# Query products of 512 columns for the last six heads of an attention layer, with the Vector engine's and the Scalar engine's work around them put in another order

## The chip, the cores and the metric

The kernel runs on one core of a Trainium2 chip. Its metric is the device time of one execution in microseconds (us), given as the median of several runs. The core has a matrix engine (PE, with its weight loads in the row PEld), a Vector engine (DVE), a Scalar engine (ACT), a GpSimd engine (POOL) and a queue that issues transfers (SP). Each takes its instructions in order and waits on semaphores for the others.

## The reference

Two pre-norm residual layers over 256 tokens of width 1024 in float32: layer 0 mixes tokens with attention, layer 1 with causal pooling, and each is followed by a squared-ReLU MLP of width 4096. The change lies in the attention of layer 0. With 256 tokens there is one block of keys, so the block choice falls away and plain causal attention is left:

```python
q, k, v = split(rms_norm(x) @ w_qkv)        # 8 heads of 128
q, k = rope(q), rope(k)                     # on the first 32 of 128 channels
p = softmax(causal(q @ k.T / sqrt(128)))
x = x + (p @ v) @ w_o
x = x + square(relu(rms_norm(x) @ w_up)) @ w_down
```

## The kernel before

**Numbers in two halves.** A float32 product is made from three products in the faster type fp32r. Each weight slab `raw` (one megabyte, 128 x 2048) is split into a high part `wh` (ACT, line 177, two pieces of 128 x 1024) and a low part `wl = raw - wh` (DVE, line 181, two pieces). The normed activations `xs` hold for each of the eight k-tiles 256 columns of high part and 256 of low part. A product is then wh·hi + wl·hi + wh·lo.

**Two forms of the product.** `chan_block` issues for a k-tile three matmuls of 256 columns into one bank of PSUM (lines 410, 411, 415). The wide form issues one of 256 columns, wl·hi (`wide_lo`, line 425), and one of 512, wh·[hi, lo] (`wide_hi`, line 432); a whole bank then holds a main term in its left half and a small term in its right half, and whoever empties the bank adds the two.

**The attention loop.** The eight heads go in four pairs, j = 0 to 3; keys and queries of a pair lie with channels on the partitions, so f = 0, 1 is the head within the pair. Before the change the keys of pairs 1 to 3 use the wide form (`key_evac`: two ACT copies of the small terms at line 615, two DVE additions at 616, a shuffle at 617, and the rotation on POOL at 620 to 622); the queries use `chan_block` and `qk_evac` (shuffle at 598 and multiplication by the cosine table at 599, both straight from PSUM, then two small operations at 601 and 602 on DVE or POOL). For j = 1, 2, 3 PE does, in this order: keys of j; within them `attend(j-2)`; `scores(j-1)`; queries of j; `prob_t(j-1)`. `scores` makes q·k, takes the negated row maxima (DVE, line 640), exponentials with sums (ACT, 648), reciprocals of the sums (DVE, 651) and scales the probabilities, those of the pair's first head on ACT (656) and of its second on DVE (659). `prob_t` transposes them on PE (670). `attend` multiplies with the values; ACT and DVE then split the output `o` into `ah` and `al` (709, 710). After the loop comes the projection with `w_o`, with `attend(2)`, `scores(3)` and `attend(3)` between its groups.

**What sets the order.** Each engine's order is the order in which the program text issues (the schedule is manual). Weight pieces are issued by `pump`, `pump_h` and `pump_l` at chosen places, one piece of `wh` on ACT and then one of `wl` on DVE. PSUM is handed round: the pool `ps_t` has two banks, taken in turn by scores `s`, transposed probabilities `pt` and outputs `o`. The scores of the second head of pair j-1 therefore wait until `al` has been read from `o` of pair j-2.

Of the kernel before, what the change touches and what calls it, by code (L numbers as in the profile page):

```python
# [11 lines left out]
F32 = mybir.dt.float32  # L12
F32R = mybir.dt.float32r
I32 = mybir.dt.int32
AF = mybir.ActivationFunctionType
ALU = mybir.AluOpType
ENG = mybir.EngineType

P = 128
SEQ = 256  # L20
# [3 lines left out]
ROT = 32  # L24
KT = D // P
NS = SEQ // P
HALF = 512
# [57 lines left out]
def tile_trunk(ctx: ExitStack, tc: tile.TileContext, x_in, positions, norm_mix, norm_mlp,  # L85
               w_qkv, w_o, pool_w, pool_scale, w_up, w_down, norm_final, consts, out):
    nc = tc.nc
# [5 lines left out]
    work = ctx.enter_context(tc.tile_pool(name="work", bufs=2))  # L93
    small = ctx.enter_context(tc.tile_pool(name="small", bufs=2))
    ps_d = ctx.enter_context(tc.tile_pool(name="ps_d", bufs=1, space=bass.MemoryType.PSUM))
    ps_u = ctx.enter_context(tc.tile_pool(name="ps_u", bufs=2, space=bass.MemoryType.PSUM))
# [90 lines left out]
    def hi_step():  # L187

        if not todo:
            i = state["next"]  # L190
            if i > min(state["cur"] + AHEAD, len(slabs) - 1):
                return False
            todo.extend(split_steps(i))
            state["next"] += 1
        step = todo.pop(0)
        step[0]()
        lows.append((state["next"] - 1, not todo, step[1]))
        return True

    def lo_step():  # L200
        if not lows:
            return False
        i, last, f = lows.pop(0)
        f()
        done[i] = done.get(i, 0) + 1
        if last:
            done[i] = 99
        return True

    def pump_h(n):  # L210
        for _ in range(n):
            hi_step()
# [5 lines left out]
    def pump(n):  # L218
        for _ in range(n):
            hi_step()  # L220
            while lows:
                lo_step()
# [182 lines left out]
    def chan_hi(acc, w, k, f, first):  # L405

        fs = slice(f * P, (f + 1) * P)
        o = acc[:, f * SEQ:(f + 1) * SEQ]
        hi = xs[:, k, 0:SEQ]
        nc.tensor.matmul(o, w[0][:, k, fs], hi, start=first, stop=False, skip_group_check=True)  # L410
        nc.tensor.matmul(o, w[1][:, k, fs], hi, start=False, stop=False, skip_group_check=True)  # L411
# [6 lines left out]
    def chan_block(acc, w, f):  # L418
        for k in range(KT):
            chan_hi(acc, w, k, f, k == 0)  # L420
            chan_lo(acc, w, k, f, k == KT - 1)

    def wide_lo(acc, w, k, f, first=True):

        nc.tensor.matmul(acc[:, 0:SEQ], w[1][:, k, f * P:(f + 1) * P], xs[:, k, 0:SEQ],  # L425
                         start=first and k == 0, stop=not first and k == KT - 1,
                         skip_group_check=True)

    def wide_hi(acc, w, k, f, first=False):


        nc.tensor.matmul(acc, w[0][:, k, f * P:(f + 1) * P], xs[:, k, :],  # L432
                         start=first and k == 0, stop=not first and k == KT - 1,
                         skip_group_check=True)
# [72 lines left out]
    for k in range(KT):  # L507
# [5 lines left out]
        for n, h in steps:  # L513
# [3 lines left out]
            for s in range(NS):  # L517
                x0 = (SEQ if n == 1 else 0) + s * P
                w = wl if n == 2 else wh
# [17 lines left out]
        if 2 <= k < 6:  # L537
# [3 lines left out]
                                 scale=1.0 / 32.0, accum_out=acc0[:, h, s:s + 1])  # L541
        if k == 5:
# [4 lines left out]
                                           op0=ALU.add, op1=ALU.add)  # L547
# [29 lines left out]
    scale = 1.0 / math.sqrt(P)  # L577
    tab = {}
# [9 lines left out]
    swap = [(i + half) % ROT for i in range(ROT)]  # L588

    def qk_bank(nm, j):  # L590
        return ps_u.tile([P, HALF], F32, tag="u", name="u_%s_%d" % (nm, j))

    def qk_evac(nm, j, u):
        ct, st = tab[nm]
        t = work.tile([P, 2, SEQ], F32, tag="X", name="t_%s_%d" % (nm, j), bufs=4)
        sw = work.tile([ROT, 2, SEQ], F32, tag="sw", name="sw_%s_%d" % (nm, j), bufs=2)
        uv = u.rearrange("p (f t) -> p f t", f=2)
        nc.vector.stream_shuffle(sw.rearrange("p f t -> p (f t)"), u[0:ROT, :], swap)
        nc.vector.tensor_tensor(t, uv, ct.broadcast_to([P, 2, SEQ]), op=ALU.mult)
        e = nc.vector if j == 0 or (nm, j) == ("q", 1) else nc.gpsimd  # L600
        e.tensor_tensor(sw, sw, st.broadcast_to([ROT, 2, SEQ]), op=ALU.mult)
        e.tensor_tensor(t[0:ROT], t[0:ROT], sw, op=ALU.add)
        return t
# [2 lines left out]
        return [ps_d.tile([P, HALF], F32, tag="d%d%d" % (f, 1 - j % 2), name="k_%d_%d" % (j, f))  # L606
                for f in range(2)]

    def key_evac(j, us):

        ct, st = tab["k"]
        t = work.tile([P, 2, SEQ], F32, tag="X", name="t_k_%d" % j, bufs=4)
        sw = work.tile([ROT, 2, SEQ], F32, tag="sw", name="sw_k_%d" % j, bufs=2)
        for f in range(2):
            nc.scalar.activation(t[:, f, :], us[f][:, SEQ:2 * SEQ], AF.Copy)
            nc.vector.tensor_tensor(t[:, f, :], us[f][:, 0:SEQ], t[:, f, :], op=ALU.add)
        nc.vector.stream_shuffle(sw.rearrange("p f t -> p (f t)"),
                                 t[0:ROT].rearrange("p f t -> p (f t)"), swap)
        e = nc.gpsimd
        e.tensor_tensor(t, t, ct.broadcast_to([P, 2, SEQ]), op=ALU.mult)  # L620
        e.tensor_tensor(sw, sw, st.broadcast_to([ROT, 2, SEQ]), op=ALU.mult)
        e.tensor_tensor(t[0:ROT], t[0:ROT], sw, op=ALU.add)
        return t

    qk = {}
    prob = {}
    mask = cst[:, C_MASK:C_MASK + 3 * P]

    def scores(j):
        q, k = qk["q", j], qk["k", j]  # L630
        pr = []
        mx = small.tile([P, 4], F32, tag="mx", name="mx_%d" % j)
        sums = small.tile([P, 4], F32, tag="sums", name="sums_%d" % j)
        for a in range(2):
            sp = ps_t.tile([P, HALF], F32, tag="t", name="s_%d_%d" % (j, a))
            nc.tensor.matmul(sp[:, 0:P], q[:, a, 0:P], k[:, a, 0:P], start=True, stop=True)
            nc.tensor.matmul(sp[:, P:3 * P], q[:, a, P:2 * P], k[:, a, :], start=True, stop=True)
            pa = work.tile([P, 3 * P], F32, tag="Y", name="p_%d_%d" % (j, a), bufs=4)
            for b, (c0, c1) in enumerate(((0, P), (P, 3 * P))):
                nc.vector.tensor_tensor_reduce(  # L640
                    pa[:, c0:c1], sp[:, c0:c1], mask[:, c0:c1], scale=-1.0, scalar=-NEG,
                    op0=ALU.add, op1=ALU.min, accum_out=mx[:, 2 * a + b:2 * a + b + 1])
            pr.append(pa)
        pump_h(1)
        for a in range(2):
            for b, (c0, c1) in enumerate(((0, P), (P, 3 * P))):
                i = 2 * a + b
                nc.scalar.activation(pr[a][:, c0:c1], pr[a][:, c0:c1], AF.Exp, scale=-1.0,
                                     bias=mx[:, i:i + 1], accum_out=sums[:, i:i + 1])
        pump_l(1)  # L650
        nc.vector.reciprocal(sums, sums)
        for a in range(2):
            for b, (c0, c1) in enumerate(((0, P), (P, 3 * P))):
                i = 2 * a + b
                if a == 0:
                    nc.scalar.activation(pr[a][:, c0:c1], pr[a][:, c0:c1], AF.Copy,
                                         scale=sums[:, i:i + 1])
                else:
                    nc.vector.tensor_scalar(pr[a][:, c0:c1], pr[a][:, c0:c1],
                                            sums[:, i:i + 1], None, op0=ALU.mult)  # L660
        prob[j] = pr

    pts = {}
# [52 lines left out]
    for j in range(4):  # L716
        w = use("k", j)
        if j == 0:
            u = qk_bank("k", j)
            chan_block(u, w, 0)  # L720
            tables()
            pump_h(2)
            v_evac(0, 0)
            v_evac(1, 0)
            chan_block(u, w, 1)
            v_evac(0, 1)
            v_evac(1, 1)
            qk["k", j] = qk_evac("k", j, u)
            pump_l(2)
        else:  # L730
            us = key_banks(j)
            for f in range(2):
                for k in range(KT):
                    wide_lo(us[f], w, k, f)
            pump(1)
            if j >= 2:
                attend(j - 2)
            for f in range(2):
                for k in range(KT):
                    wide_hi(us[f], w, k, f)  # L740
            qk["k", j] = key_evac(j, us)
            scores(j - 1)
        w = use("q", j)
        u = qk_bank("q", j)
        chan_block(u, w, 0)
        pump(1 if j else 2)
        chan_block(u, w, 1)
        qk["q", j] = qk_evac("q", j, u)
        if j == 0:
            pump(1)  # L750
        if j == 3:
            nc.scalar.activation(vh, vsb[:, 0, HALF:D], AF.Copy)
            nc.vector.tensor_tensor(vl, vsb[:, 0, HALF:D], vh.bitcast(F32), op=ALU.subtract)
        if j >= 1:
            prob_t(j - 1)
        pump(1)
# [10 lines left out]
    w = use("o", 0)  # L767
# [6 lines left out]
    w = use("o", 1)  # L774
# [4 lines left out]
    w = use("o", 2)  # L779
# [414 lines left out]
```

## Time and profile before

| what | us |
|---|---|
| median of 3 runs (lowest, highest) | 485.41 (484.21, 485.72) |
| time of the profiled execution | 484.62 |
| its span in the profile | 482.5 |
| PE busy | 474.7 |
| DVE busy | 338.8 |
| ACT busy | 255.1 |
| POOL busy | 43.1 |

The profiled execution is 0.8 us below the median, and 2.1 us of its time lie outside the span. In a row of the timeline the first number is the start in us from the span's start, the second the duration; then come engine, line, operation, output and inputs with their sizes, and in brackets the idle time before it with what ended it. A PE row's duration overlaps the next row's, since matmuls are pipelined; the distance of two starts is what a matmul costs.

### The profile page before, as it was taken

To read this page: it belongs to the slowest core of one execution; us is meant where nothing else is said; L and a number is where in the kernel's file an instruction comes from. 1 tells how busy PE (TensorE), PEld (TensorE's weight loads), DVE (VectorE), ACT (ScalarE), POOL (GpSimd) and SP (SyncE) were. 2 spreads that over 40 slices of the span, in tenths; PEclk is the share of its full clock that TensorE was granted. 3 is DMA by queue.
4 is the path that set the end of the run, shared out by engine and by line. 5 is a ranking of instruction groups with operands and counts; after the bars stand their busy time and mean duration, and the time that the engine had idled before them with its cause. 6 is when DMAs were issued, how large, how long until landed. Compare 5 with 4: busy or idle time off the path is not lost.

```text
span 482.5 us, 6552 instructions
## 1 busy us (share of the span) xinstructions
PE 474.7 (98%) x2570; PEld 412.1 (85%) x2570; DVE 338.8 (70%) x498; ACT 255.1 (53%) x418; POOL 43.1 (9%) x41
## 2 busy tenths in 40 slices
PE   8999999999999999999999999999999999999994
PEld 7789999888888888888888889888888888888884
DVE  4789998955877484848566687778756557484745
ACT  4696665653686272635355554476535446272523
POOL 6910456300000000000000000000000000000000
PEclk9999999999999999999999999999999999999999
DMA  7986643480477758556573570078747472736202
GB/s 266 349 280 223 196 174 123 143 259 1 124 251 236 263 196 282 186 163 219 170 249 147 175 261 2 18 248 297 239 135 277 139 252 97 262 120 230 88 1 87
DMA packets 57342, 89.58 MB, mean 186 GB/s; under 512 B 2944, under 2 KB 46048, under 8 KB 57312
## 3 DMA queue, kind: packets, MB, share of 16 engines
q1 hardware_dynamic: 56896, 88.72, 55.1%
q8 instruction: 20, 0.33, 0.3%
q10 hardware_dynamic: 416, 0.45, 0.3%
q14 instruction: 10, 0.08, 0.0%
HBM read 88.11 MB, written 1.05 MB: 185 GB/s over the span
## 4 chain that ended last, share of the span: by engine, by line
PE 97%; DMA 1%; SPq 0%; ACT 0%; DVE 0%; issue 0%; ACTq 0%
PE u_m L432 24%; PE u_m L425 13%; PE d_m L401 12%; PE d_m L402 12%; PE d_m L403 12%; PE d_v L520 4%; PE k L432 2%; PE u_q L411 2%; PE u_q L410 2%; PE u_q L415 2%; PE d_o L401 2%; PE d_o L403 2%; PE d_o L402 2%; DMA xt<-in_x_dram 1%; PE k L425 1%; PE d_p L1066 1%
## 5 line engine op out<-in xcount | busy, mean ns | idle before, releaser
L432 PE MATMUL u_m<-xs,wh_u 128*128 128x512 f32 x512 | 122.1, 390 | 0.0
L432 PEld LDWEIGHTS u_m<-xs,wh_u 128*128 128x128 f32 x512 | 94.7, 188 | 18.8
L401 PE MATMUL d_m<-wh_d,hh 128*128 128x512 f32 x252 | 98.1, 389 | 0.0
L402 PE MATMUL d_m<-wl_d,hh 128*128 128x512 f32 x252 | 98.0, 389 | 0.0
L403 PE MATMUL d_m<-wh_d,hl 128*128 128x512 f32 x252 | 98.0, 389 | 0.0
L181 DVE TENSOR_TENSOR wl_d<-raw_d,wh_d 128x1024 fp32r<-128x1024 f32 x64 | 76.2, 1221 | 17.0 <-ACT wh_d L177 17.0
L181 DVE TENSOR_TENSOR wl_u<-raw_u,wh_u 128x1024 fp32r<-128x1024 f32 x64 | 75.8, 1222 | 12.2 <-ACT wh_u L177 12.2
L177 ACT ACTIVATE wh_d<-raw_d 128x1024 fp32r<-128x1024 f32 x64 | 64.7, 1046 | 21.7 <-DMA raw_d<-in_mlp_w_down_dram 21.7
L799 ACT ACTIVATE t<-u_m 128x256 f32<-128x256 f32 x64 | 24.0, 378 | 83.8 <-PE u_m L425 54.6
L177 ACT ACTIVATE wh_u<-raw_u 128x1024 fp32r<-128x1024 f32 x64 | 63.9, 1046 | 7.1 <-DMA raw_u<-in_mlp_w_up_dram 7.1
L425 PEld LDWEIGHTS u_m<-xs,wl_u 128*128 128x128 f32 x512 | 64.0, 191 | 1.4
L425 PE MATMUL u_m<-xs,wl_u 128*128 128x256 f32 x512 | 64.9, 283 | 0.0
L800 DVE TENSOR_TENSOR t<-u_m,t 128x256 f32<-128x256 f32 x64 | 26.5, 422 | 53.9 <-ACT t L799 53.2
L403 PEld LDWEIGHTS d_m<-wh_d,hl 128*128 128x128 f32 x252 | 47.3, 188 | 9.8
L401 PEld LDWEIGHTS d_m<-wh_d,hh 128*128 128x128 f32 x252 | 47.3, 188 | 9.8
L402 PEld LDWEIGHTS d_m<-wl_d,hh 128*128 128x128 f32 x252 | 47.3, 188 | 9.8
L810 ACT ACTIVATE hh<-hf 128x512 fp32r<-128x512 f32 x32 | 20.2, 633 | 45.0 <-DVE hf L809 45.0
L811 DVE TENSOR_TENSOR hl<-hf,hh 128x512 fp32r<-128x512 f32 x32 | 22.2, 692 | 22.5 <-ACT hh L810 22.5
L809 DVE SCALAR_TENSOR_TENSOR hf<-t 128x512 f32<-128x512 f32 x32 | 22.1, 692 | 1.1
L410 PE MATMUL u_q<-xs,wh_q 128*128 128x256 f32 x64 | 18.6, 291 | 0.0
L411 PE MATMUL u_q<-xs,wl_q 128*128 128x256 f32 x64 | 18.1, 283 | 0.0
L415 PE MATMUL u_q<-xs,wh_q 128*128 128x256 f32 x64 | 18.1, 283 | 0.0
(218 smaller groups left out, 554.8 us busy)
## 6 DMA issues: line engine op xcount, KB each, us to landing
raw_u<-in_mlp_w_up_dram SPq DMA_DIRECT2D x32, 1024.0 KB, 6.3
raw_d<-in_mlp_w_down_dram SPq DMA_DIRECT2D x32, 1024.0 KB, 4.8
raw_o<-in_attn_w_o_dram SPq DMA_DIRECT2D x4, 1024.0 KB, 4.8
raw_k<-in_attn_w_qkv_dram SPq DMA_DIRECT2D x4, 768.0 KB, 5.2
raw_q<-in_attn_w_qkv_dram SPq DMA_DIRECT2D x4, 768.0 KB, 4.8
raw_v<-in_attn_w_qkv_dram SPq DMA_DIRECT2D x2, 1024.0 KB, 9.0
raw_v<-in_attn_w_qkv_dram SPq DMA_DIRECT2D x3, 512.0 KB, 7.1
raw_k<-in_attn_w_qkv_dram SPq DMA_DIRECT2D x4, 256.0 KB, 5.4
```

Of the source, the lines that this page charges most:

```text
L177: nc.scalar.activation(wh[:, sl], src[:, sl], AF.Copy)
L181: nc.vector.tensor_tensor(wl[:, sl], src[:, sl], wh[:, sl].bitcast(F32), op=ALU.subtract)
L401: nc.tensor.matmul(acc, lh, wh, start=first, stop=False)
L402: nc.tensor.matmul(acc, lh, wl, start=False, stop=False)
L403: nc.tensor.matmul(acc, ll, wh, start=False, stop=last)
L410: nc.tensor.matmul(o, w[0][:, k, fs], hi, start=first, stop=False, skip_group_check=True)
L411: nc.tensor.matmul(o, w[1][:, k, fs], hi, start=False, stop=False, skip_group_check=True)
L415: nc.tensor.matmul(acc[:, f * SEQ:(f + 1) * SEQ], w[0][:, k, fs], xs[:, k, SEQ:2 * SEQ], start=False, stop=last, skip_group_check=True)
L425: nc.tensor.matmul(acc[:, 0:SEQ], w[1][:, k, f * P:(f + 1) * P], xs[:, k, 0:SEQ], start=first and k == 0, stop=not first and k == KT - 1, ...
L432: nc.tensor.matmul(acc, w[0][:, k, f * P:(f + 1) * P], xs[:, k, :], start=first and k == 0, stop=not first and k == KT - 1, skip_group_che ...
L799: nc.scalar.activation(t[:, ts], u[:, SEQ:2 * SEQ], AF.Copy)
L800: nc.vector.tensor_tensor(t[:, ts], u[:, 0:SEQ], t[:, ts], op=ALU.add)
```

## The change

The queries of pairs 1 to 3 are made in the wide form, into two banks, and emptied by a new function `query_evac` in the way of the keys. ACT's copies of the small terms are in a function of their own (`small_terms`). In `scores(j-1)` the row maxima now come first on DVE, and the additions and shuffle of the keys of pair j, which stood ahead of them, follow (the argument `between`). The probabilities of both heads of a pair are scaled on ACT.

```diff
+    def small_terms(nm, j, us):
+        t = work.tile([P, 2, SEQ], F32, tag="X", name="t_%s_%d" % (nm, j), bufs=4)
+        for f in range(2):
+            nc.scalar.activation(t[:, f, :], us[f][:, SEQ:2 * SEQ], AF.Copy)
+        return t
+
-    def key_evac(j, us):
+    def key_evac(j, us, t):
...
-        t = work.tile([P, 2, SEQ], F32, tag="X", name="t_k_%d" % j, bufs=4)
         sw = work.tile([ROT, 2, SEQ], F32, tag="sw", name="sw_k_%d" % j, bufs=2)
         for f in range(2):
-            nc.scalar.activation(t[:, f, :], us[f][:, SEQ:2 * SEQ], AF.Copy)
             nc.vector.tensor_tensor(t[:, f, :], us[f][:, 0:SEQ], t[:, f, :], op=ALU.add)
...
+    def query_evac(j, us):
+
+        ct, st = tab["q"]
+        t = small_terms("q", j, us)
+        sw = work.tile([ROT, 2, SEQ], F32, tag="sw", name="sw_q_%d" % j, bufs=2)
+        for f in range(2):
+            nc.vector.tensor_tensor(t[:, f, :], us[f][:, 0:SEQ], t[:, f, :], op=ALU.add)
+        nc.vector.stream_shuffle(sw.rearrange("p f t -> p (f t)"),
+                                 t[0:ROT].rearrange("p f t -> p (f t)"), swap)
+        nc.vector.tensor_tensor(t, t, ct.broadcast_to([P, 2, SEQ]), op=ALU.mult)
+        e = nc.vector if j == 1 else nc.gpsimd
+        e.tensor_tensor(sw, sw, st.broadcast_to([ROT, 2, SEQ]), op=ALU.mult)
+        e.tensor_tensor(t[0:ROT], t[0:ROT], sw, op=ALU.add)
+        return t
...
-    def scores(j):
+    def scores(j, between=None):
...
             pr.append(pa)
+        if between is not None:
+            between()
         pump_h(1)
...
-                if a == 0:
-                    nc.scalar.activation(pr[a][:, c0:c1], pr[a][:, c0:c1], AF.Copy,
-                                         scale=sums[:, i:i + 1])
-                else:
-                    nc.vector.tensor_scalar(pr[a][:, c0:c1], pr[a][:, c0:c1],
-                                            sums[:, i:i + 1], None, op0=ALU.mult)
+                nc.scalar.activation(pr[a][:, c0:c1], pr[a][:, c0:c1], AF.Copy,
+                                     scale=sums[:, i:i + 1])
...
-            qk["k", j] = key_evac(j, us)
-            scores(j - 1)
+            t = small_terms("k", j, us)
+            scores(j - 1, lambda: qk.update({("k", j): key_evac(j, us, t)}))
         w = use("q", j)
-        u = qk_bank("q", j)
-        chan_block(u, w, 0)
-        pump(1 if j else 2)
-        chan_block(u, w, 1)
-        qk["q", j] = qk_evac("q", j, u)
         if j == 0:
...
+        else:
+            us = [ps_u.tile([P, HALF], F32, tag="u", name="q_%d_%d" % (j, f)) for f in range(2)]
+            for f in range(2):
+                for k in range(KT):
+                    wide_lo(us[f], w, k, f)
+            pump(1)
+            for f in range(2):
+                for k in range(KT):
+                    wide_hi(us[f], w, k, f)
+            qk["q", j] = query_evac(j, us)
```

On the Vector engine, at the scores of pair 0 in the turn of j = 1, the additions for the keys `t_k` (from the PSUM banks `k_0`, `k_1`) stand ahead of the maxima `mx` of the scores `s`. Before:

```order
L616 TENSOR_TENSOR t_k_587<-k_0_549,t_k_587 128x256
L616 TENSOR_TENSOR t_k_587<-k_1_550,t_k_587 128x256
L617 STREAM_SHUFFLE sw_k_588<-t_k_587 32x512
L640 ISA p_0_602,mx_597<-s_0_599,cst 128x128
L640 ISA mx_597 128x1
```

At the same place now:

```order
L659 ISA p_1_601,mx_590<-s_1_598,cst 128x256
L659 ISA mx_590 128x1
L620 TENSOR_TENSOR t_k_587<-k_0_549,t_k_587 128x256
L620 TENSOR_TENSOR t_k_587<-k_1_550,t_k_587 128x256
L621 STREAM_SHUFFLE sw_k_604<-t_k_587 32x512
```

The three operations for the keys moved behind all the maxima of the pair.

The Vector engine again, directly behind that: the second piece of the low weights of the queries of pair 2 (`wl_q`), the reciprocals, the first piece for the keys of pair 3 (`wl_k`), and the emptying of the queries of pair 1. Before:

```order
L181 TENSOR_TENSOR wl_q_568<-raw_q_473,wh_q_567 128x1024
L651 RECIPROCAL sums_598<-sums_598 128x4
L659 TENSOR_SCALAR p_1_608<-p_1_608,sums_598 128x128
L659 TENSOR_SCALAR p_1_608<-p_1_608,sums_598 128x256
L181 TENSOR_TENSOR wl_k_650<-raw_k_507,wh_k_649 128x1024
L598 STREAM_SHUFFLE sw_q_678<-u_q_624 32x512
L599 TENSOR_TENSOR t_q_677<-u_q_624,ct_q 128x512
L601 TENSOR_TENSOR sw_q_678<-sw_q_678,st_q 32x512
L602 TENSOR_TENSOR t_q_677<-t_q_677,sw_q_678 32x512
```

At the same place now:

```order
L181 TENSOR_TENSOR wl_q_568<-raw_q_473,wh_q_567 128x1024
L672 RECIPROCAL sums_591<-sums_591 128x4
L181 TENSOR_TENSOR wl_k_643<-raw_k_507,wh_k_642 128x1024
L635 TENSOR_TENSOR t_q_662<-q_0_624,t_q_662 128x256
L635 TENSOR_TENSOR t_q_662<-q_1_625,t_q_662 128x256
L636 STREAM_SHUFFLE sw_q_665<-t_q_662 32x512
L638 TENSOR_TENSOR t_q_662<-t_q_662,ct_q 128x512
L640 TENSOR_TENSOR sw_q_665<-sw_q_665,st_q 32x512
L641 TENSOR_TENSOR t_q_662<-t_q_662,sw_q_665 32x512
```

The two scalings are gone, two additions came in, and the shuffle and the multiplication read SBUF where they read PSUM.

On the Scalar engine, at the same place of the turn of j = 1, from the scaling of the probabilities `p` on. Before:

```order
L656 ACTIVATE p_0_602<-p_0_602,sums_598 128x128
L656 ACTIVATE p_0_602<-p_0_602,sums_598 128x256
L177 ACTIVATE wh_k_649<-raw_k_507 128x1024
L681 ACTIVATE pts_0_687<-pt_0_683 128x384
L681 ACTIVATE pts_1_693<-pt_1_689 128x384
```

At the same place now:

```order
L676 ACTIVATE p_0_595<-p_0_595,sums_591 128x128
L676 ACTIVATE p_0_595<-p_0_595,sums_591 128x256
L676 ACTIVATE p_1_601<-p_1_601,sums_591 128x128
L676 ACTIVATE p_1_601<-p_1_601,sums_591 128x256
L177 ACTIVATE wh_k_642<-raw_k_507 128x1024
L612 ACTIVATE t_q_662<-q_0_624 128x256
L612 ACTIVATE t_q_662<-q_1_625 128x256
L698 ACTIVATE pts_0_676<-pt_0_672 128x384
L698 ACTIVATE pts_1_682<-pt_1_678 128x384
```

Two more scalings stand ahead of the weight piece `wh_k`, and two copies of query terms stand between it and the copies `pts` of the transposed probabilities. In the turns of j = 2 and 3 the three places look alike, with pieces of `w_o` for those of the keys; there the last two operations of the query emptying are on POOL, before and now.

More of the change, by code (lines that the diff above doesn't have):

```diff
@@ L740, in tile_trunk @@
                     wide_hi(us[f], w, k, f)
-            qk["k", j] = key_evac(j, us)
-            scores(j - 1)
+            t = small_terms("k", j, us)
+            scores(j - 1, lambda: qk.update({("k", j): key_evac(j, us, t)}))
         w = use("q", j)
-        u = qk_bank("q", j)
-        chan_block(u, w, 0)
-        pump(1 if j else 2)
-        chan_block(u, w, 1)
-        qk["q", j] = qk_evac("q", j, u)
-        if j == 0:
-            pump(1)
+        if j == 0:
+            u = qk_bank("q", j)
+            chan_block(u, w, 0)
+            pump(2)
+            chan_block(u, w, 1)
+            qk["q", j] = qk_evac("q", j, u)
+            pump(1)
+        else:
[8 more added lines that the diff above has]
+            qk["q", j] = query_evac(j, us)
         if j == 3:
```

## Prediction

> **What bounds the kernel now.** First I read the busy times and the chain that ended last.
>
> ```profile
> PE 474.7 (98%) x2570; PEld 412.1 (85%) x2570; DVE 338.8 (70%) x498; ACT 255.1 (53%) x418; POOL 43.1 (9%) x41
> PE 97%; DMA 1%; SPq 0%; ACT 0%; DVE 0%; issue 0%; ACTq 0%
> ```
>
> PE is the bound, over the whole span. Next, whom PE waited for:
>
> ```profile
> PE warm_up L298 <- DVE warm L237: 1.1, 1, 1.1
> PE tr_a L318 <- DMA xt<-in_x_dram: 0.5, 1, 0.5
> ```
>
> Both waits lie before 10 us. Behind them PE never waits, so the change can gain only what it takes off PE's own work, and loses every wait that it opens. Whether one opens is read from the stage it touches:
>
> ```profile
> 55.40:70.10 14.70, 14.70 (x105) 13.83 (x104) 13.96 (x26) 8.85 (x21) 5.82 (x4) 1.00 0.51 185
> ```
>
> This is the turn of j = 2 (columns: stretch, length, busy PE, PEld, DVE, ACT, POOL, then the granted clock): DVE is busy 13.96 of 14.70 us. Over the span it has 30% to spare, here 5%; I therefore follow DVE's queue.
>
> **The change on PE.**
>
> ```profile
> 49.12 0.28 PE L411 MATMUL u_q<-xs,wl_q 128*128 128x256 f32 x1
> ...
> 54.62 0.28 PE L415 MATMUL u_q<-xs,wh_q 128*128 128x256 f32 x1
> ```
> ```profile
> 55.64 1.92 PE k L425 x16
> ...
> 58.87 3.66 PE k L432 x16
> ```
>
> These are the second and the last of the 48 query matmuls of pair 1: 46 steps in 5.50 us, 0.1196 us each, 5.74 for 48. The wide form does the same for keys in 1.92 + 3.66 = 5.58 (chain, 16 of each). Gain 0.16 a turn, 0.5 us over three. Emptying into two banks costs PE nothing: the turn between two query blocks covers it.
>
> **The change on DVE, turn of j = 1.**
>
> ```profile
> 49.68 0.74 DVE L616 TENSOR_TENSOR t_k<-k,t_k 128x256 f32<-128x256 f32 x2
> ...
> 50.46 0.72 DVE L617 STREAM_SHUFFLE sw_k<-t_k 32x512 f32<-32x512 f32 x1
> 51.09 0.26 DVE L640 CUSTOM_DVE_ANT_0 p<-s,cst 128x128 f32<-128x128 f32 x1
> ...
> 52.18 1.46 DVE L181 TENSOR_TENSOR wl_q<-raw_q,wh_q 128x1024 fp32r<-128x1024 f32 x1
> ...
> 53.77 1.38 DVE L659 TENSOR_SCALAR p<-p,sums 128x128 f32<-128x128 f32 x2
> 55.55 1.81 DVE L181 TENSOR_TENSOR wl_k<-raw_k,wh_k 128x1024 fp32r<-128x1024 f32 x1 [0.41 <-ACT wh_k L177]
> ...
> 57.29 0.72 DVE L598 STREAM_SHUFFLE sw_q<-u_q 32x512 f32<-32x512 f32 x1
> 57.92 0.66 DVE L599 TENSOR_TENSOR t_q<-u_q,ct_q 128x512 f32<-128x512 f32 x1
> ...
> 59.21 0.68 DVE L602 TENSOR_TENSOR t_q<-t_q,sw_q 32x512 f32<-32x512 f32 x1
> 59.82 1.21 DVE L181 TENSOR_TENSOR wl_k<-raw_k,wh_k 128x1024 fp32r<-128x1024 f32 x1
> ...
> 62.09 0.67 DVE L710 TENSOR_TENSOR al<-o,ah 128x512 fp32r<-128x512 f32 x1
> ```
> ```profile
> 51.27 1.29 POOL L620 TENSOR_TENSOR t_k<-t_k,ct_k 128x512 f32<-128x512 f32 x1 [16.38 <-DVE sw_k L617]
> 52.52 2.27 POOL L621 TENSOR_TENSOR sw_k<-sw_k,st_k 32x512 f32<-32x512 f32 x1
> 54.86 1.41 POOL L622 TENSOR_TENSOR t_k<-t_k,sw_k 32x512 f32<-32x512 f32 x1
> ...
> 71.29 1.28 POOL L601 TENSOR_TENSOR sw_q<-sw_q,st_q 32x512 f32<-32x512 f32 x1 [1.83 <-DVE sw_q L598]
> ```
> ```profile
> 53.77 0.80 ACT L656 ACTIVATE p<-p,sums 128x128 f32<-128x128 f32 x2 [0.51 <-DVE sums L651]
> 54.47 1.04 ACT L177 ACTIVATE wh_k<-raw_k 128x1024 fp32r<-128x1024 f32 x1
> ```
>
> DVE and POOL take turns. The `wl_q` piece starts at 52.18, POOL's first operation ends at 52.56, the piece 1.08 later (53.64); POOL's second, begun at 52.52, ends 1.15 after that (54.79), though such an operation takes 1.28 alone. The `wl_k` piece of 55.55 ends 1.09 after POOL's third (56.27). What began first goes first, the other waits for its end.
>
> The Trainium skill (page "SBUF — State Buffer", section "SBUF: two separate sides") says that GpSimd and a Vector operation with two SBUF inputs hold a shared port pair exclusively for the whole instruction, the first to start winning. The trace agrees (1.08 and 1.09 us after the other's end). Were the port shared by halves instead, `wl_k` would start at once and last at most its 1.81 us, some 0.5 late in place of 1.0, and the sum below would be nearer +3.6 than +5.0.
>
> The maxima put first shift the pieces, not their sum: `wl_q` is again at 52.18. POOL's first operation, now released only by the shuffle's end there, comes behind it, so the piece takes about 1.22 and ends at W = 53.40. Then:
> - ACT starts 0.13 after W (53.64 to 53.77), scales four pieces in 1.40 instead of two in 0.70 (53.77 to 54.47), makes `wh_k` in 1.04; DVE may begin `wl_k` 0.04 later, W + 2.61 = 56.01. Its own scaling (1.38) is gone, but DVE only idles in its place.
> - POOL's three: W + 1.15 to 1.29, 1.24 more (1.28 less the 0.04 overlap of 52.56 and 52.52), 0.07 between (54.79 to 54.86): the third starts at W + 2.46 to 2.60, up to 0.15 us ahead of `wl_k`. POOL first is likelier; `wl_k` then waits for 1.28 us of POOL and is about 1.0 late. DVE first: nothing lost.
> - Queued behind `wl_k` on DVE are the emptying of the queries, two weight pieces and `al`; for `al` PE waits.
> - The queries' emptying took 57.29 to 59.82, 2.53 us. Now: additions 0.78 (49.68 to 50.46), shuffle 0.75, multiplication 0.60 to 0.63, two small ones 1.31: 3.44. The multiplication reads SBUF now; its bounds are 0.66 (PSUM) and the 0.69 of
>
> ```profile
> L809 DVE SCALAR_TENSOR_TENSOR hf<-t 128x512 f32<-128x512 f32 x32 | 22.1, 692 | 1.1
> ```
>
> So the operation behind `wl_k` starts at 57.15 (DVE first) or 58.17 (POOL first) instead of 57.29; after 3.44 of emptying and 2.27 of two weight pieces (59.82 to 62.09) `al` ends at 63.53 or 64.55 instead of 62.76. That matters because of one moment on PE:
>
> ```profile
> 54.74 0.90 PE L670 MATMUL pt<-ident,p 128*128 128x128 f32 x6
> ...
> 63.02 0.39 PE L636 MATMUL s<-t_k,t_q 128*128 128x128 f32 x2
> 63.24 0.60 PE L637 MATMUL s<-t_k,t_q 128*128 128x256 f32 x2
> ```
>
> The second head's scores (63.02) take the PSUM bank that `al` empties; 63.02 less 62.76 leaves a slack of 0.26 us. PE comes 0.16 earlier, at 62.86, and waits **0.7 or 1.7 us**.
>
> Two smaller delays in this turn I set at nothing. The transposes of the probabilities (54.74, now about 54.58) need the last scaled piece near the end of their 0.65 us; ACT has it at W + 0.13 + 1.5 = 55.0, so PE waits between 0 and 0.1. ACT's query copies stand ahead of `pts`, which only `attend` of the next turn reads, some 2.8 us after the transposes begin; that covers them, and if it didn't it would be 0.2 at most.
>
> **Turns of j = 2 and 3.**
>
> ```profile
> 66.94 1.38 DVE L659 TENSOR_SCALAR p<-p,sums 128x128 f32<-128x128 f32 x2
> ...
> 70.48 0.73 DVE L598 STREAM_SHUFFLE sw_q<-u_q 32x512 f32<-32x512 f32 x1
> ...
> 71.80 4.09 DVE L181 TENSOR_TENSOR wl_o<-raw_o,wh_o 128x1024 fp32r<-128x1024 f32 x2
> 75.81 0.68 DVE L710 TENSOR_TENSOR al<-o,ah 128x512 fp32r<-128x512 f32 x1
> ...
> 85.03 0.72 DVE L598 STREAM_SHUFFLE sw_q<-u_q 32x512 f32<-32x512 f32 x1
> ...
> 87.95 0.74 DVE L676 TENSOR_TENSOR ptp<-pt,ptp 128x256 fp32r<-128x256 f32 x2
> ```
> ```profile
> 77.61 0.38 PE L636 MATMUL s<-t_k,t_q 128*128 128x128 f32 x2
> ...
> 88.80 0.60 PE L693 MATMUL o<-pts,vsb 128*128 128x128 f32 x4
> ```
>
> From `al`'s end to the next W lie 3.9 us (0.9 for PE's second head, 0.35 its last maximum, 0.78 + 0.64 for the keys, 1.22 for the piece). W comes at 67.4 or 68.4, the operation behind `wl_o` at W + 3.74 (71.15) or W + 4.77 (73.2) against 70.48. From there to `al`'s end it was 6.01 (to 76.49); additions and order add 0.8, a multiplication that now takes turns with POOL about 0.4: 7.2. `al` ends at 78.35 or 80.4; PE arrives at 77.61 - 0.32 + 0.7 (1.7) = 78.0 or 79.0: wait **0.4 or 1.4**.
>
> In turn 3 W is at 82.2 or 84.3, the next operation at 85.95 or 89.05 (85.03 before). The split `ptp` ended 3.66 later (88.69), now 4.8: 90.7 or 93.8. `attend(2)`, whose slack was 0.11, arrives at 88.80 - 0.48 + 1.1 (3.1) = 89.4 or 91.4: wait **1.3 or 2.4**. Later DVE waits for PE again,
>
> ```profile
> 106.97 0.69 DVE L792 TENSOR_TENSOR xt<-d_o,xt 128x512 f32<-128x512 f32 x1 [2.78 <-PE d_o L403]
> ```
>
> so nothing more is lost, nor given back.
>
> **Sum.** POOL first: 1.7 + 1.4 + 2.4 - 0.5 = +5.0. DVE first: 0.7 + 0.4 + 1.3 - 0.5 = +1.9. Both stand against the profiled execution, 484.62; the median lies 0.8 higher, which I leave inside the range. Forecast: 489.6.
>
> **Rivals.**
> 1. DVE wins the turns: +1.9, 486.5. For it: the margin is between 0.15 us and nothing. If the three turns differ, about +3.
> 2. No slower: the scaling taken from DVE (1.38) pays for the longer emptying (0.91), and `al` ends before 62.86, with all waits gone: 484.62 - 0.5 = 484.1. It decides if `wl_k` can start by about W + 1.9, as at 55.55. Against it: ACT's queue has the four scalings in front of `wh_k`, 0.70 us more.
> 3. Clearly faster, by 1.5 us and more: PE's matmuls of 512 columns would have to save three times what the keys' rows show. Nothing speaks for it.
>
> **How the numbers follow.** POOL first 0.50, mixed turns 0.13, rival 1 0.17, rival 2 0.17, rival 3 0.03. About 0.3% (1.5 us) is what a measurement can tell from no change. Slower: 0.50 + 0.13 and 0.10 of rival 1 = 0.73; same: 0.07 + 0.17 = 0.24; faster 0.03. The range leaves out rivals 2 and 3: from 485.2, below rival 1 with its waits a little smaller, to 491.2, the forecast with the median's 0.8 and POOL's longer times. Within the likeliest case alone I would say 488.4 to 491.2.
>
> **What would show it.** Right: PE idle before the second head's scores in turns 2 and 3 and before `attend(2)`, released by DVE; DVE idle over 2 us behind each reciprocal, released by ACT's weight piece; POOL's third operation starting just ahead of `wl_k`. Wrong: PE without waits and 0.5 us shorter, or a gap at the transposes of the probabilities, which I put at under 0.3 us.

## The result, and the profile after

The kernel after takes 491.62 us (median of 6 executions, 490.13 to 492.38) against 485.27 (6, 484.21 to 485.72) of the kernel before beside it: a ratio of 1.0134, 95% interval 1.0113 to 1.0154. It is slower, by more than forecast: 489.6 was said, with a range that ended at 491.2. The profiled execution took 490.13, 5.5 us more than that of before, where the sum had said 5.0.

The busy times and the chain that ended last, of the kernel after:

```profile
PE 475.2 (97%) x2522; PEld 408.5 (84%) x2522; DVE 336.2 (69%) x496; ACT 259.3 (53%) x432; POOL 41.6 (9%) x41
PE 86%; DVE 8%; ACT 2%; DMA 2%; issue 1%; SPq 0%; DVEq 0%; ACTq 0%
```

PE's busy time is nearly that of before (474.7), so the 5.5 us are not work of PE; DVE now holds 8% of the chain. Whom PE waited for (us in total, times, longest), without the waits before 10 us:

```profile
PE s L655 <- DVE al L727: 2.4, 2, 1.6
PE o L710 <- DVE ptp L693: 2.1, 1, 2.1
...
PE s L655 <- POOL t_q L641: 0.6, 1, 0.6
```

The timeline has them in these places (the idle time before a row stands in brackets):

```profile
64.26 0.49 PE L655 MATMUL s<-t_k,t_q 128*128 128x128 f32 x2 [1.61 <-DVE al L727]
...
78.91 0.49 PE L655 MATMUL s<-t_k,t_q 128*128 128x128 f32 x2 [0.62 <-POOL t_q L641]
...
80.59 0.49 PE L655 MATMUL s<-t_k,t_q 128*128 128x128 f32 x2 [0.76 <-DVE al L727]
...
93.97 0.71 PE L710 MATMUL o<-pts,vsb 128*128 128x128 f32 x4 [2.11 <-DVE ptp L693]
```

And the turn in which they arise, DVE, then POOL, then ACT:

```profile
51.82 1.20 DVE L181 TENSOR_TENSOR wl_q<-raw_q,wh_q 128x1024 fp32r<-128x1024 f32 x1
52.94 0.16 DVE L672 RECIPROCAL sums<-sums 128x4 f32<-128x4 f32 x1
55.61 2.25 DVE L181 TENSOR_TENSOR wl_k<-raw_k,wh_k 128x1024 fp32r<-128x1024 f32 x1 [2.52 <-ACT wh_k L177]
57.78 0.74 DVE L635 TENSOR_TENSOR t_q<-q,t_q 128x256 f32<-128x256 f32 x2
...
63.53 0.67 DVE L727 TENSOR_TENSOR al<-o,ah 128x512 fp32r<-128x512 f32 x1
```
```profile
51.99 2.17 POOL L624 TENSOR_TENSOR t_k<-t_k,ct_k 128x512 f32<-128x512 f32 x1 [17.75 <-DVE sw_k L621]
54.13 1.28 POOL L625 TENSOR_TENSOR sw_k<-sw_k,st_k 32x512 f32<-32x512 f32 x1
55.49 1.29 POOL L626 TENSOR_TENSOR t_k<-t_k,sw_k 32x512 f32<-32x512 f32 x1
```
```profile
53.13 1.50 ACT L676 ACTIVATE p<-p,sums 128x128 f32<-128x128 f32 x4 [1.66 <-DVE sums L672]
54.54 1.04 ACT L177 ACTIVATE wh_k<-raw_k 128x1024 fp32r<-128x1024 f32 x1
```

W, the end of the `wl_q` piece, is 53.02. ACT scales until 54.6 and only then makes `wh_k`; DVE idles 2.52 us; POOL's third operation begins at 55.49, 0.12 ahead of `wl_k`, which therefore lasts 2.25 us instead of 1.20. The emptying of the queries begins at 57.78. The same picture stands in the other two turns (`wl_o` at 71.09 and at 87.43; each takes 2.25 us and stands behind 2.51 of idleness).

### The profile page after: what moved, and what is told of

Same layout as the page of the kernel before. It is cut to its first block, busy times and chain, and to the rows that moved or that the text cites. A ratio compares the mean times of both kernels' runs of the same rounds, so it can differ in the third digit from the quotient of the medians.

```text
span 488.1 us, 6474 instructions
## 1 busy us (share of the span) xinstructions
PE 475.2 (97%) x2522; PEld 408.5 (84%) x2522; DVE 336.2 (69%) x496; ACT 259.3 (53%) x432; POOL 41.6 (9%) x41
## 3 DMA queue, kind: packets, MB, share of 16 engines
HBM read 88.11 MB, written 1.05 MB: 183 GB/s over the span
## 4 chain that ended last, share of the span: by engine, by line
PE 86%; DVE 8%; ACT 2%; DMA 2%; issue 1%; SPq 0%; DVEq 0%; ACTq 0%
PE u_m L432 24%; PE u_m L425 13%; PE d_m L403 12%; PE d_m L401 12%; PE d_m L402 12%; PE d_v L520 5%; DVE wl_o L181 2%; DVE wl_k L181 2%; PE d_o L401 1%; PE d_o L403 1%; PE d_o L402 1%; DVE wl_q L181 1%; DMA raw_q<-in_attn_w_qkv_dram 1%; ACT p L676 1%; PE pb L1010 1%
## 5 line engine op out<-in xcount | busy, mean ns | idle before, releaser
L181 DVE TENSOR_TENSOR wl_o<-raw_o,wh_o 128x1024 fp32r<-128x1024 f32 x8 | 14.3, 1797 | 5.3 <-ACT wh_o L177 5.3
L520 PE MATMUL d_v<-wh_v,xs 128*128 128x512 f32 x64 | 16.8, 400 | 0.3 <-ACT wh_v L177 0.2
L364 ACT ACTIVATE junk<-xt 128x512 f32<-128x512 f32 x15 | 9.5, 630 | 13.9 <-DVE xt L821 13.5
```

Source lines behind the costliest of these rows:

```text
L181: nc.vector.tensor_tensor(wl[:, sl], src[:, sl], wh[:, sl].bitcast(F32), op=ALU.subtract)
L520: nc.tensor.matmul(dv[s, h], xs[:, k, x0:x0 + P], w[:, k % 2, hs], start=k == 0 and n == 0, stop=k == KT - 1 and n == 2)
```

## The experiments

Each ratio is to runs of the kernel before on the same chip. The theory: DVE is late at the queries' emptying, because behind each reciprocal it waits for ACT's weight piece and then for POOL, and the longer emptying leaves nothing to make it up; PE pays for it in three places. The chief rival: the wide products in two banks are the cost themselves.

### Undoing what makes DVE late

**e1: the weight piece ahead of the scalings** (against after).

```diff
         nc.vector.reciprocal(sums, sums)
+        if between is not None:
+            pump_h(1)
         for a in range(2):
...
                     wide_lo(us[f], w, k, f)
-            pump(1)
+            pump_l(1)
```

(The second place is the one between the two passes of the queries.)

> The kernel after with one thing moved: ScalarE's piece of the next slab (wh_k in the first block) is issued between the exponentials and the four scalings, where ScalarE idles 1.66 us in the trace, instead of behind the scalings. Nothing else differs. Theory (DVE's 2.5 us of idleness behind each reciprocal is what makes DVE late, and PE waits 1.9 + 1.9 + 2.4 us for it): wl_k begins right behind the reciprocal, some 2.5 us earlier against W, the three waits fall to under 0.5 us together, and the gain of the wide queries (0.55) is left: 484.5 to 485.8 us, a ratio to before of 0.998 to 1.002. Rival (the wide products in two banks and the longer emptying are the cost, whatever DVE does behind the reciprocal): the waits at the scores and at attend(2) stay near their size, 489.5 us or more, ratio 1.009 or more.

Measured: 486.05 us, ratio 1.0025 (1.0016 to 1.0034), 0.25 us above the theory's range and far from the rival's 489.5. The edit did not do quite what was written of it: weight pieces may run only three slabs ahead, so in the first block nothing could be issued at the new place and `wl_k` came behind the emptying; in the other two blocks a `wl` piece directly follows the reciprocal. In all three the emptying now begins 1.83 us behind the reciprocal's end, instead of 4.68. What is left of PE's waits:

```profile
PE o L712 <- DVE ptp L695: 0.6, 1, 0.6
...
PE s L655 <- DVE al L729: 0.2, 1, 0.2
```

So of the 6.5 us above before (1.34% of 484.7) 1.3 are left: some 5.2 us go with DVE's lateness, while the wide products and their two banks are unchanged.

**e2: without POOL's third operation on the keys** (against after; line 626 is left out, so the keys lack one term).

```diff
-        e.tensor_tensor(t[0:ROT], t[0:ROT], sw, op=ALU.add)
```

> The kernel after without POOL's third operation on the keys (t_k plus sw_k, 32x512), so the rotated part of the keys lacks its second term. Nothing else differs. Theory (that operation, 0.12 us ahead of wl_k in each of the three blocks, holds wl_k up by 1.04 us): wl_k takes 1.20 us and not 2.25, still 2.5 us behind the reciprocal, and each of the three waits falls by about 1.0: 488.2 to 489.2 us against 491.6, ratio 1.006 to 1.008. Rival (DVE's lateness comes from ScalarE alone, the meeting with POOL lies beside other work): the waits stay, 491 to 492 us, ratio 1.012 or more.

Measured: 487.20 us, ratio 1.0052 (1.0038 to 1.0065), a larger fall than the theory's. DVE's idleness is that of after, but the piece is not held up (the timeline, then PE's waits):

```profile
56.13 1.23 DVE L181 TENSOR_TENSOR wl_k<-raw_k,wh_k 128x1024 fp32r<-128x1024 f32 x1 [2.51 <-ACT wh_k L177]
```
```profile
PE s L654 <- DVE al L726: 1.2, 2, 0.6
PE o L709 <- DVE ptp L692: 1.1, 1, 1.1
```

PE's waits at these places fall from 5.1 to 2.3 us in the trace, as expected, and the two profiled executions lie 2.7 us apart (490.13 and 487.41). The medians lie further apart because the median of after is 1.5 us above its profiled execution, which the part on the prediction takes up.

**e3: one scaling of four back on DVE** (against after).

```diff
-                nc.scalar.activation(pr[a][:, c0:c1], pr[a][:, c0:c1], AF.Copy,
-                                     scale=sums[:, i:i + 1])
+                if i != 2:
+                    nc.scalar.activation(pr[a][:, c0:c1], pr[a][:, c0:c1], AF.Copy,
+                                         scale=sums[:, i:i + 1])
+                else:
+                    nc.vector.tensor_scalar(pr[a][:, c0:c1], pr[a][:, c0:c1],
+                                            sums[:, i:i + 1], None, op0=ALU.mult)
```

> The kernel after with one of the four scalings (the second head's 128 columns) on DVE again, behind the reciprocal where DVE idles. ScalarE's piece then ends about 0.35 to 0.40 us earlier, so wl_k can begin near W+2.2 us, ahead of POOL's third operation at W+2.47. Theory (who begins first has the turn): wl_k takes 1.20 us and DVE is through at W+3.4 instead of W+4.84, each wait falls by about 1.4: 487 to 488 us, ratio 1.0035 to 1.0065. Rival (the order of beginning does not decide, POOL's operation goes first or the two share): DVE gains only the 0.4 us, each wait falls by 0.4 at most: 490 to 491.2 us, ratio 1.009 to 1.012.

Measured: 486.38 us, ratio 1.0041 (1.0028 to 1.0055); 1.65 us above before. The turns change hands:

```profile
55.59 1.23 DVE L181 TENSOR_TENSOR wl_k<-raw_k,wh_k 128x1024 fp32r<-128x1024 f32 x1 [1.07 <-ACT wh_k L177]
...
55.76 2.19 POOL L626 TENSOR_TENSOR t_k<-t_k,sw_k 32x512 f32<-32x512 f32 x1
```

DVE's piece begins 0.17 us ahead and takes 1.23; now POOL's operation takes 2.19. ACT's piece comes 0.3 us sooner against W, and the emptying begins 1.3 us sooner (W + 3.45 instead of W + 4.76). This kernel is close to the prediction's first rival: +1.9 was worked out for it.

**e4: the outputs in another bank** (against after).

```diff
-        o = ps_t.tile([P, HALF], F32, tag="t", name="o_%d" % j)
+        o = (ps_d if j < 2 else ps_t).tile([P, HALF], F32, tag="d0%d" % (j % 2) if j < 2 else "t",
+                                           name="o_%d" % j)
```

> The kernel after with the outputs of attend(0) and attend(1) in a bank of ps_d that the previous keys have left, instead of the ps_t bank that the second head's scores want next. Nothing else differs; DVE does the same work in the same order. Theory (DVE is late, the bank is only where PE meets it): the waits of the second head's scores for al (1.9 and 1.0) go, but PE then meets the late DVE elsewhere, at the third block's first scores (t_q, 1.5 or so) and at attend(2) (2.4 to 2.7): 489.6 to 491 us, ratio 1.008 to 1.012. Rival (the ring of two ps_t banks is the cost): the two waits go for good, 2.9 us less: 488.9 us or less, ratio 1.0075 or less.

Measured: 490.31 us, ratio 1.0108 (1.0092 to 1.0124): the theory's case. The waits for `al` are gone and PE meets the late DVE further on:

```profile
PE o L711 <- DVE ptp L693: 2.6, 1, 2.6
PE s L655 <- POOL t_q L641: 1.4, 1, 1.4
```

### One part of the change at a time

These start from the kernel before. e5 takes the new query branch with `query_evac` alone; e6 `between` alone; e7 the scalings alone; e8 is the kernel after without the third part (e5 and e6 together).

The core of e5, of e6 and of e7, in this order:

```diff
-        qk["q", j] = qk_evac("q", j, u)
...
+            for f in range(2):
+                for k in range(KT):
+                    wide_hi(us[f], w, k, f)
+            qk["q", j] = query_evac(j, us)
```
```diff
-            qk["k", j] = key_evac(j, us)
-            scores(j - 1)
+            t = small_terms("k", j, us)
+            scores(j - 1, lambda: qk.update({("k", j): key_evac(j, us, t)}))
```
```diff
-                else:
-                    nc.vector.tensor_scalar(pr[a][:, c0:c1], pr[a][:, c0:c1],
-                                            sums[:, i:i + 1], None, op0=ALU.mult)
...
+                nc.scalar.activation(pr[a][:, c0:c1], pr[a][:, c0:c1], AF.Copy,
+                                     scale=sums[:, i:i + 1])
```

e8 takes the last of these back in the kernel after.

> The kernel before with one part of the change alone: the queries of the last six heads by 512-column products and their longer emptying; maxima behind the keys' additions and the second head's scaling on DVE, as before. Theory (the products gain some 0.55 us, and their emptying makes DVE later by 0.9 us a block; this alone exceeds DVE's slack by a little): waits of 0.5 to 0.9 us at the second head's scores in two blocks and at attend(2), about 2.0 in sum, less the gain: 485.5 to 487 us, ratio 1.002 to 1.005. Rival (the wide products and their two banks are what costs): nearly all of it is here, 489 us or more, ratio 1.009 or more.

> The kernel before with one part alone: maxima ahead of the keys' additions, so that the keys' operations on DVE and then on POOL come about 1 us later against the exponentials; narrow queries and the second head's scaling on DVE as before. Theory: POOL's operations now meet DVE's scalings and wl_k, DVE is back some 1 us later, most of which the slack before the queries' emptying takes up; the transposes of the probabilities may wait once for about 1.3: 484.5 to 486.3 us, ratio 1.000 to 1.0035. Rival (the new order by itself is the cost): 488 us or more, ratio 1.007 or more.

> The kernel before with one part alone: all four scalings on ScalarE. DVE then idles some 2.5 us behind each reciprocal for ScalarE's piece of the next slab, as in the kernel after; but POOL's key operations, started before the maxima, are through when wl_k begins, and the short emptying leaves room. Theory (idleness costs only where POOL's operation and the longer emptying come on top): no wait of PE above 0.3 us, 484.2 to 485.4 us, ratio 0.999 to 1.0015. Rival (the scalings on ScalarE cost by themselves, wherever the rest stands): waits of 1 us or more in each block, 487 us or more, ratio 1.005 or more.

> The kernel after with the second head's two scalings on DVE again, behind the reciprocal; the wide queries and the new order of the maxima stay. ScalarE's piece ends 0.9 us earlier, but DVE's scalings now stand ahead of wl_k and meet POOL's operations. Theory: DVE is through about 3.7 us behind W instead of 4.84, each of the three waits is 0.8 to 1.2 instead of 1.9 to 2.4, and the transposes of the probabilities may wait once for about 1.3: 486.5 to 488.3 us, ratio 1.004 to 1.0075, between e5_wide_only and the kernel after. Rival (the scaling's place does not matter): 490.5 us or more, ratio 1.011 or more.

| kernel | median us | ratio to before (95%) |
|---|---|---|
| e5, wide queries | 486.75 | 1.0045 (1.0031 to 1.0059) |
| e6, maxima first | 485.15 | 1.0011 (1.0001 to 1.0021) |
| e7, scalings on ACT | 484.47 | 0.9999 (0.9988 to 1.0009) |
| e8, e5 and e6 | 486.88 | 1.0049 (1.0032 to 1.0065) |

All four times came as the theory had them, and no part alone is the culprit: 2.2, 0.5 and 0.0 us, where all three cost 6.5. In the traces PE waits 0.59, 0.31 and 0.79 us at the three places in e5, once 0.90 at the transposes in e6, nowhere in e7, and 0.37 and 0.89 at two of the three places and 0.85 at the transposes in e8. The row that shows best why is from e7:

```profile
55.91 1.23 DVE L181 TENSOR_TENSOR wl_k<-raw_k,wh_k 128x1024 fp32r<-128x1024 f32 x1 [2.51 <-ACT wh_k L177]
```

The very idleness of 2.51 us that is so dear in the kernel after is here, and costs nothing: POOL's key operations started before the maxima and are through, `wl_k` takes 1.23, and the short emptying leaves room. The parts are dear together: the scalings make the hole, the order of the maxima puts POOL's third operation at its end, and the longer emptying takes the room in which DVE would have caught up. This account is put together from e2, e3, e7 and e8; the scalings with only one of the other two parts were not run. e2, which has the hole and the longer emptying without POOL at the hole's end, stands at 1.0052, near e5's 1.0045.

### The clock behind a wait

The trace of e4 had a row that no step of the prediction had foreseen: behind the wait for `ptp` the granted clock (of PE) stood at 0.50 for some 3.4 us. The mean clock of e4's executions went with their time (0.993 and 0.994 at 491.1; 0.997 and 0.998 at 489.5 and 489.1). e10 to e12 follow that up. e10 is the kernel after again; e11 and e12 are the kernel before with one delay on DVE ahead of the third split of probabilities (six and four splits of the upper value rows; the diff is e11's):

```diff
-            nc.vector.tensor_tensor(vl, vsb[:, 0, HALF:D], vh.bitcast(F32), op=ALU.subtract)
+            for _ in range(6):
+                nc.vector.tensor_tensor(vl, vsb[:, 0, HALF:D], vh.bitcast(F32), op=ALU.subtract)
```

> The kernel after, unchanged, with more executions than the first time. Theory (in some executions the granted clock falls to half for some 3.3 us after one of PE's waits, as the trace of e4_obank shows behind attend(2); that costs about 1.7 us and lowers the mean clock of the span from about 0.998 to 0.994): the times fall into two groups, near 490 to 491.3 us at a mean clock of 0.996 or more and near 491.5 to 492.5 at 0.995 or less. Rival (the times scatter for other reasons, as those of before do): one group, and the mean clock does not go with the time.

> The kernel before with the split of the upper value rows (vl, 128x512, on DVE) written six times instead of once, so that DVE reaches the split of the third block's probabilities late and PE waits at attend(2) for about 3.6 us; nothing else differs. Theory (a wait of this length halves the granted clock for some 3.3 us afterwards): before plus 3.6, plus 0.3 to start again, plus 1.7 for the clock in nearly every execution: 489.3 to 490.8 us, ratio 1.010 to 1.013, mean clock 0.995 or less, half the clock behind the wait in the trace. Rival (the clock does not go with waiting): 487.8 to 488.8 us, ratio 1.007 to 1.009, mean clock as before.

> The same with four splits, so that PE waits at attend(2) for about 2.2 us, as in the kernel after, and nowhere else. Theory (at this length the clock falls in some executions and not in others): times in two groups, 486.6 to 487.4 us at the mean clock of before and about 1.7 us more at 0.995 or less. Rival (the clock falls at any wait of 2 us): all at 488.3 us or more; or (it falls only after some 3 us of waiting): all at 486.6 to 487.4.

e10: 491.46 us, ratio 1.0143 (1.0126 to 1.0159). With the first six there are ten executions of the kernel after: five at a mean clock of 0.994 (491.93, 491.93, 491.99, 492.27, 492.38) and five at 0.997 or 0.998 (490.13, 490.13, 491.00, 491.23, 491.24). The groups don't overlap; their means lie 1.35 us apart. Both executions of after that were profiled are of the second group, with the clock full behind waits of 2.1 us, so the low clock itself was not seen in a trace of after.

e11: 490.89 us, ratio 1.0135 (1.0121 to 1.0149), mean clock 0.991 to 0.994 in all four executions. PE waits 4.1 us instead of the 3.6 expected, and the time is 0.1 us above the theory's range and 2.1 above the rival's. e12: 489.42 us, ratio 1.0107 (1.0092 to 1.0121). Its wait came out at 2.6 us, not 2.2, and the two groups expected for it did not appear: all four stand at 0.992 to 0.994. These are PE's wait in e12, and the stretches behind it (the number ahead of the DMA share is the granted clock):

```profile
91.89 0.71 PE L693 MATMUL o<-pts,vsb 128*128 128x128 f32 x4 [2.60 <-DVE ptp L676]
```
```profile
92.00:93.00 1.00, 1.00 (x8) 1.00 (x9) 1.00 (x2) 0.00 (x0) 0.00 (x0) 0.87 0.00 0
93.00:94.00 1.00, 1.00 (x6) 0.90 (x5) 0.30 (x1) 0.29 (x1) 0.00 (x0) 0.50 0.00 0
94.00:95.00 1.00, 1.00 (x4) 0.81 (x3) 0.67 (x1) 1.00 (x2) 0.00 (x0) 0.50 0.33 85
95.00:96.00 1.00, 1.00 (x3) 0.74 (x3) 0.74 (x2) 1.00 (x2) 0.00 (x0) 0.50 0.82 220
96.00:97.00 1.00, 1.00 (x8) 0.92 (x7) 0.57 (x2) 0.19 (x1) 0.00 (x0) 0.93 0.98 312
```

If the clock is either 1.00 or 0.50, it is low for 0.26 + 3.00 + 0.14 = 3.40 us, beginning 0.85 us after PE had resumed. Read in the same way, e4 has it low for 3.40 us from 0.05 us after PE's return, and e11 for 6.8 us from 1.7 us before it. In these three traces PE had idled for 2.4 to 2.6 of the 3.4 us ahead of the fall; in the two traces of after, where the clock stayed full, for 2.1 at most. Waiting and a low clock go together, then, by the mean clocks: at 1.1 us never (e2, four executions at 0.996 or more), at 2.1 in half the executions of after, at 2.6 in six of eight (e4 and e12), at 4.1 always. The waits are those of the one or two traces of each kernel. e11 and e12 differ from before by the delay alone, so the wait is the cause there; why the same wait lowers the clock in one execution and not in another stays open.

### Whether the wide queries gain

**e9: e1, e4 and the value split moved** (against e1; the bank of e4 also in it, and the split now ahead of `query_evac`).

```diff
-        if j == 3:
+            if j == 1:
                 nc.scalar.activation(vh, vsb[:, 0, HALF:D], AF.Copy)
                 nc.vector.tensor_tensor(vl, vsb[:, 0, HALF:D], vh.bitcast(F32), op=ALU.subtract)
```

> The kernel of e1_piece_ahead with two moves more: attend(0) and attend(1) write the bank that the previous keys have left (as in e4_obank), and the split of the upper value rows (vh on ScalarE, vl on DVE) stands in the first wide block, where DVE waits 1.8 us for ScalarE, instead of the third. Theory (the 1.3 us that e1_piece_ahead is above the kernel before are its two waits left, 0.2 and 0.6 us with some 0.3 each to start again, less nothing): no wait of PE above 0.2 us at the second head's scores or attend(2), and the gain of the wide queries shows: 483.8 to 484.8 us, ratio 0.998 to 1.000. Rival (the wide queries gain nothing to speak of, or cost elsewhere): 485.2 us or more, ratio 1.001 or more.

Measured: 484.63 us against 484.37, ratio 1.0004 (0.9995 to 1.0013). PE's waits at the scores and at attend are gone, but no gain can be measured; the interval takes in both cases. The trace says more: the first scores of the first and of the fourth pair, in before and in e9:

```profile
47.69 0.38 PE L636 MATMUL s<-t_k,t_q 128*128 128x128 f32 x2
...
91.33 0.38 PE L636 MATMUL s<-t_k,t_q 128*128 128x128 f32 x2
```
```profile
47.80 0.38 PE L655 MATMUL s<-t_k,t_q 128*128 128x128 f32 x2
...
90.94 0.38 PE L655 MATMUL s<-t_k,t_q 128*128 128x128 f32 x2
```

43.64 us between them became 43.14: the 0.5 of the sum. Up to attend(3), at 101.52 and 101.29, only 0.34 is left, because DVE still idled behind the fourth reciprocal.

**e13: the piece ahead there too** (against e9).

```diff
-        if between is not None:
-            pump_h(1)
+        pump_h(1)
```

> The kernel of e9_three_moves with ScalarE's piece ahead of the scalings in the fourth pair as well, where it was left behind them. Theory (the wide queries gain 0.5 us up to the fourth pair's scores, and DVE's 2.5 us behind the fourth reciprocal give half of it back at attend(3)): attend(3) starts 53.3 to 53.4 us behind the first pair's scores instead of 53.49 (before 53.83), and the time is 0.2 to 0.3 us below e9_three_moves: 0.1 to 0.6 us below before, ratio 0.9987 to 0.9998. Rival (the gain ends in a later wait whatever attend(3) does): attend(3) starts earlier and the time is not below before, ratio 1.000 or more.

Measured: 484.54 us against 484.44, ratio 0.9994 (0.9985 to 1.0003). attend(3) stands 53.39 us behind the first scores (101.83 less 48.44), as the theory had it (before: 53.83). Of these 0.44 us another 0.2 are lost ahead of the pooling products near 288 us, where the second of two squares on ACT follows the first 0.2 us later than in before; that this is the cause was not tried, nor why it does so in e9 and e13. No kernel here beats the kernel before by what can be measured.

## Why the prediction was right, and where it was wrong

Right was the mechanism, step by step. Up to the change, the trace of after runs 0.40 us ahead of that of before (first scores at 47.29 against 47.69; PE's wait of 0.5 us for the input before 10 us is missing), so W = 53.02 is the forecast's 53.40. Forecast for ACT's start, POOL's third and `wl_k`: W + 0.13, + 2.46 to 2.60, + 2.61; measured + 0.11, + 2.47, + 2.59. `wl_k` was 1.0 late, the emptying took 3.48 (57.78 to 61.26; forecast 3.44), `al` ended at 64.20 (forecast 64.55, less 0.40). The waits fell at the three places named, and the transposes of the probabilities did not gain one. The Trainium skill's rule (page "SBUF — State Buffer", section "SBUF: two separate sides": who starts first has the shared ports for the whole instruction) holds in both directions: after and e3 differ in who is 0.12 to 0.17 us ahead, and the other loses 0.9 to 1.05.

Rival 1 was well sized (+1.9 against e3's 1.65). Rival 2's condition, `wl_k` by W + 1.9, points the right way, but its limit was not tried: e1 went far beyond it (the emptying itself began at W + 1.9) and nearly all waits were gone, e3 fell short of it (`wl_k` at W + 2.3) and kept waits of 0.8 us (two together) and 0.9. Rival 3 found no support: the wide queries gain 0.5 us (e9), as the keys' rows had shown.

Wrong were two sizes:

1. **The sum: +5.0, measured +5.7** on PE's rows of the chain from the first scores to the first MLP products (64.23 us in before, 69.96 after). The gain was 0.5, as said, and `attend(2)` cost 2.4, as said, with PE's arrival and DVE's `ptp` both 0.6 to 0.7 us later than said. Mis-sized were the first wait, 1.7, which made the following scores 1.87 us late (1.61 of idleness, and 0.26 for PE to run down and start again), and above all the second, **1.4 against 1.93**. The failed step there is "from `al`'s end to the next W lie 3.9 us": it was 4.30 (64.20 to 68.50), because the last maximum ended 1.66 behind `al` and not 1.25. The prediction left only the last maximum (0.35) for after PE's scores; both maxima of the second head came there (0.64), and PE, starting from idle, took 1.02 instead of 0.9:

```profile
65.22 0.29 DVE L659 CUSTOM_DVE_ANT_0 p<-s,cst 128x128 f32<-128x128 f32 x1 [0.46 <-PE s L656]
...
65.44 0.42 DVE L659 CUSTOM_DVE_ANT_0 p<-s,cst 128x256 f32<-128x256 f32 x1
```

The remaining 0.1 or so goes with starting again. A releaser was missed too: POOL's `t_q` held up the first head by 0.62 before `al` held up the second; `al` alone set when the second head could start.

2. **The step from the profiled execution to the median: 0.8 allowed in the range, 1.5 measured.** Either size alone would have left the median inside (484.62 + 5.0 + 1.5 = 491.1; 490.13 + 0.8 = 490.9); the two together put it outside. The 1.5 has two parts. The profiled execution was the quickest of the six: e10's, the same kernel at the same full clock, took 0.87 more, and 0.86 of it was there at the first scores (48.15 against 47.29), since PE waited for the input ahead of everything that was changed:

```profile
10.00 0.63 PE L318 MATMUL tr_a<-ident,xt 128*128 128x128 f32 x4 [1.11 <-DMA xt<-in_x_dram]
```

The other part is the clock. In half of the executions its mean is lower and they take 1.35 us more; by e4, e11 and e12 that is a stretch at half the clock behind a long wait, though no trace of after shows it. With 1.35 taken off those three of the six, the median would be 491.0 (an estimate): some 0.9 is the first part, which the 0.8 covers, and some 0.6 the clock. The prediction put the clock's part at nothing: it looked at the clock of before (1.00), where PE never waits after 10 us, and took it for a constant. A forecast that opens a wait of 2.4 us should have priced what the wait does to the clock as well.

## What to carry to other kernels

Before moving work from one engine to another, look at what stands behind it on the receiving engine's queue: here 0.7 us more of scalings on ACT delayed its weight piece by as much (`wl_k` at W + 2.59 instead of W + 1.91), and the meeting with POOL that followed made DVE 1.1 us later at the queries' emptying (W + 4.76 instead of W + 3.65). Whether an idle stretch costs anything is decided by what comes between it and the next moment at which the bounding engine needs the result; the same 2.5 us were free in e7 and dear in the kernel after, so the parts of a change must also be priced together. A wait of PE cost more than its idle time here, some 0.3 us to start again, and from 2.1 us on, in some executions, a lower clock as well.

## What the hardware showed that was not expected

The half clock behind a wait: 0.50 for 3.40 us behind a wait of 2.6 us in e12. The Trainium skill (page "TensorE: Matmul & The Clock Gate", section "Part 1: The HAM clock gate (the "warmup" mystery)") says that the clock is halved after an idle window of about 3.4 us that runs freely. The half clock and the length agree; but the same page's rule, in "HAM oscillation — how this bites in real kernels", to avoid gaps of PE over some 3.4 us, is too generous here: 2.6 us of waiting was enough in six of eight executions (by the mean clock; seen in the traces of e4 and e12), and at 2.1 us half of them ran with the lower mean clock. That the free-running window decides which executions are hit would fit, and no run here shows it.
